# A hybrid recurrent decoder layer on one core: shared buffers, a parameter chain on another engine, and three products or splits moved in the order

## Chip, cores and metric

The kernel runs on one core of a Trainium2 chip. The metric is the device time of one execution in microseconds (us); lower is better. Kernels are compared by the median of several runs.

## The reference, cut to what matters

One layer is computed for 544 tokens of 1024 features in float32: 32 tokens of a sample group (8 sequences of 4) and 512 of a prompt. All the work is on x transposed, features on partitions and tokens along the row.

```python
z = x @ w_in                                   # columns: xa, ya, sb, sc, sh, us, gl
xa_c = conv4(xa);  gx, ga = sigmoid(gates(xa_c))
a = exp(-8 * ga * softplus(-lam)); bx = sqrt(1 - a*a) * gx * xa_c
out_a = (scan(a, bx) * gelu(ya)) @ proj_a      # RG-LRU
out_b = (sb * conv3(sc * sh)) @ proj_b         # short convolution
abar = exp(step * (a_re + i*a_im))             # needs exp, cos, sin of the parameters
y = Re(C @ scan(abar, B @ us)) + d * us        # SSM: 32 groups, 64 complex states each
zc = gelu(y)
out_c = (zc * sigmoid(zc @ glu_w + glu_b)) @ proj_c
m = sum over the branches of sigmoid(gl) * out
x = LN(alpha*x + m @ w_out);  x = LN(alpha*x + relu(x @ up)**2 @ down)
```

## The kernel before

Every float32 product is made of three products of rounded halves: a weight block w is split into wh (a cast on ScalarE, lines 114 and 836) and wl = w - wh (VectorE, lines 115 and 837), the input likewise, and TensorE adds wh.xh, wh.xl and wl.xh (line 146). A tile of z is 128 output features: 48 matmuls over 8 blocks of input features and two halves of the tokens. Weights come by DMA on SyncE's queue into three raw buffers (`rawp`) and, split, into four pairs (`wp`); the split of a block is written two tiles ahead of its product.

Large intermediate tiles come from one pool of 14 equal buffers (`slot`, function `stile`); a new tile waits until the buffer that it is given has been read for the last time. Rows for a single tile (`ttile`) share four buffers and products four PSUM buffers (`big`). The program is written in order for all engines, and a planner then orders each engine's own queue: an instruction that its estimate finds ready may go ahead of an earlier one that is not. On the chip each queue then runs strictly in that order. GpSimd and VectorE operations of all helpers show line 238 (`tt`), 242 and 244 (`ts`).

The first stage computes us, then runs a counter `ti` over the tiles of z: 0 to 7 xa and ya in turn, 8 to 11 sb, 12 to 19 sc and sh in turn; 20 to 27 are the tiles of the merge of branch B (`merge_b`), and 28 on those of branch A (`merge7`, which for most pairs of gate tiles uses seven half-size products instead of eight, `pair7`, with sums of weight blocks on GpSimd and sums of x, `Tt0`). After tile `ti` the side work listed for that number is written (`at`, `run_side`):

- 0: `params_ssm`, the SSM parameters on GpSimd: an exponential of 16 columns, sine and cosine of 128 columns (8 angles), then the small tables A and F; 1: `etable`, which doubles a table E of 128 powers seven times, with factors cn and sn out of the scratch tile scr. 1 to 4: `u_move`, DMAs that bring us_t into the layout U.
- 2 to 9: `a_gate` and `a_rec`, 9 to 12 `a_sqrt` and `a_coef`, 13 `a_scan`, 14 to 17 `a_out`: the RG-LRU.
- for each of eight SSM units u: `ssm_w` and `ssm_o` (weights, GpSimd) ahead, `ssm_a` (transposes) at UA, `ssm_b` at UB = UA + 1 (input product, then scans on VectorE with E, then states HP on GpSimd), `ssm_c` at UC = UA + 2 (output product, reads HP).
- 30 to 33: `z_move`, DMAs that bring the SSM outputs Y into zc.

sb is copied from PSUM into its tile sbt by ScalarE (line 718); the copies must be made before the PSUM buffers can be used again. Before branch A's merge, GpSimd subtracts halves of x in place (`t_sum`, into xq), and four `t_put` calls split the results into the Tt tiles. After it comes the GLU of branch C: zh and zl split zc, two products of glu_w, tanh (th), a product with zt = zh + zl, and a split into ch and cl; then branch C's merge, w_out and the MLP, which the change leaves as they are.

Of the kernel before, what the change touches and what calls it, by code (L numbers as in the profile page):

```python
# [33 lines left out]
RAHEAD = 2  # L34
W2 = 1
AH1 = 4
UA = [13, 15, 17, 19, 21, 22, 24, 25]
UB = [a + 1 for a in UA]
UC = [a + 2 for a in UA]
K4_FIRST = {"a": (3,), "c": ()}  # L40


# [22 lines left out]
def kernel(ctx: ExitStack, tc: tile.TileContext, I, O):  # L65
# [171 lines left out]
    def tt(e, o, a, b, op):  # L237
        e.tensor_tensor(o, a, b, op=op)  # L238
# [75 lines left out]
        ts(V, hb[:, 8:12], C("glb"), 0.5, None, MUL)  # L314
        P["hb"] = hb

    def params_ssm():
        step, dn = P["step"], P["dn"]
        mag = stemp(16)
        va = stemp(16)  # L320
        tt(G, va, step, C("are"), MUL)
        precise_exp(G, mag, va, 16, "e1")
        ang = stemp(128).rearrange("p (f j) -> p f j", f=8)
        tt(G, ang[:, 0], step, C("aim"), MUL)
        for m in range(7):
            ts(G, ang[:, m + 1], ang[:, 0], float(4 << m), None, MUL)
        angf = ang.rearrange("p f j -> p (f j)")
        kk = stemp(128)
        t4 = stemp(128)
        ts(G, kk, angf, 2.0 / math.pi, MAGIC, MUL, ADD)  # L330
        ts(G, kk, kk, MAGIC, None, SUB)
        c1 = float(np.float32(int(math.pi / 2 * 2048) / 2048.0))
        c2_ = math.pi / 2 - c1
        e2 = 2.0 ** (math.floor(math.log2(c2_)) - 11)
        c2v = math.floor(c2_ / e2) * e2
        c3 = c2_ - c2v
        for c in (c1, c2v, c3):
            fma(G, angf, kk, -c, angf, t4)
        r2 = stemp(128)
        snf, cnf = stemp(128), stemp(128)  # L340
        sn, cn = (x.rearrange("p (f j) -> p f j", f=8) for x in (snf, cnf))
        tt(G, r2, angf, angf, MUL)
        f = [1.0 / math.factorial(i) for i in range(13)]
        ts(G, snf, r2, f[9], -f[7], MUL, ADD)
        for c in (f[5], -f[3], 1.0):
            tt(G, snf, snf, r2, MUL)
            ts(G, snf, snf, c, None, ADD)
        tt(G, snf, snf, angf, MUL)
        ts(G, cnf, r2, -f[10], f[8], MUL, ADD)
        for c in (-f[6], f[4], -f[2], 1.0):  # L350
            tt(G, cnf, cnf, r2, MUL)
            ts(G, cnf, cnf, c, None, ADD)
        ts(G, t4, kk, 0.25, MAGIC, MUL, ADD)
        ts(G, t4, t4, MAGIC, None, SUB)
        ta, tb = stemp(128), stemp(128)
        fma(G, kk, t4, -4.0, kk, ta)
        ts(G, ta, kk, 0.0, 2.0, ALU.max, MUL)
        tt(G, t4, ta, kk, SUB)
        ck = stemp(128)
        ts(G, ck, t4, -1.0, 1.0, MUL, ADD)  # L360
        ts(G, t4, t4, -1.0, 2.0, MUL, ADD)
        tt(G, kk, kk, t4, MUL)
        tt(G, ta, snf, kk, MUL)
        tt(G, tb, cnf, kk, MUL)
        tt(G, cnf, cnf, ck, MUL)
        tt(G, cnf, cnf, ta, SUB)
        tt(G, snf, snf, ck, MUL)
        tt(G, snf, snf, tb, ADD)
# [36 lines left out]
        P.update(A_r=A_r, A_i=A_i, F_r=F_r, F_i=F_i, rho=rho, cn=cn, sn=sn)  # L405

    def etable():
        E_r = stile(shape=(128, 16, 128), name="E_r")
# [135 lines left out]

    def z_move(jj):
        if not ZC:
            ZC.append(stile(shape=(128, 4, 4, NCH), name="zc"))
        zc = ZC[0]
        for s in range(4):
            nc.sync.dma_start(out=zc[32 * jj:32 * jj + 32, :, s], in_=YT[0][32 * s:32 * s + 32, jj:16:4])  # L550

# [81 lines left out]
                S.activation(AQ["r"][:, ct], aT[:, ct], AF.Identity, bias=one[:, 0:1], scale=-1.0)  # L633

    def a_sqrt():
        AQ["q"] = stile(name="q")
        S.activation(AQ["q"], aT, AF.Sqrt, scale=-1.0)

    def a_rec(ct):
        r = AQ["r"][:, ct]  # L640
# [1 line left out]
        tt(V, bx[:, ct], bx[:, ct], r, MUL)  # L642

    def a_coef(ct):
        S.activation(aT[:, ct], AQ["r"][:, ct], AF.Identity, bias=one[:, 1:2], scale=2.0)
        tt(V, bx[:, ct], bx[:, ct], AQ["q"][:, ct], MUL)

    def a_scan():
        tm = s1.tile([128, 4, NB], F32, tag="tm", name="tm")
        prev = C("slh").rearrange("p (c b) -> p c b", c=4)  # L650
        for s in range(4):
            tt(V, tm, aT[:, :, s:TS:4], prev, MUL)
            prev = bx[:, :, s:TS:4]
            tt(V, prev, tm, prev, ADD)
        V.tensor_copy(st_lh[:, :, 0:NB], prev)
        for ct in range(4):
            V.tensor_tensor_scan(bx[:, ct, TS:T], aT[:, ct, TS:T], bx[:, ct, TS:T], 0.0, op0=MUL, op1=ADD)
        V.tensor_copy(st_lh[:, :, NB:NB + 1], bx[:, :, T - 1:T])

    def a_out(ct):  # L660
# [8 lines left out]
    def at(i, f, *a):  # L669
        side.setdefault(i, []).append((f, a))  # L670
# [17 lines left out]
    for ct in range(4):  # L688
# [1 line left out]
        at(2 * ct + 3, a_rec, ct)  # L690
        at(9 + ct, a_coef, ct)
        at(14 + ct, a_out, ct)
    at(0, params_ssm)
    at(1, etable)
    side[9].insert(0, (a_sqrt, ()))
    at(13, a_scan)
    at(UB[7], ssm_state)
# [13 lines left out]
        run_side(ti)  # L711
        ti += 1

    sbt = stile(name="sbt")
    for ct in range(4):
        ps = big()
        z_tile(outs_flat(ps))
# [68 lines left out]
        d, e, f = (x[:, :, n] for x, n in (d, e, f))  # L786
        tt(G, d, e, f, SUB)

    def t_puts():
        a, b = xq  # L790
        return [t_put(x[:, :, n]) for x, n in ((a, N1), (b, N2), (a, N2), (b, N1))]

    def t_make(x):
        sr = srp.tile([128, 2, 4, H2], F32, tag="sr", name="sr")
# [78 lines left out]
    def pair7(X, Tt):  # L873
# [14 lines left out]
        prod(P2, Wa, 512, [x[:, :, N1] for x in X[1]])  # L888
        done(Wa)
        tt(V, t[0][:, N1], P2, p1, ADD)  # L890
        Ws = take()
        P6 = mk()
        prod(P6, Ws, 512, Tx(1))
# [47 lines left out]
    def merge7(kh, kl, k4f, pl, out=None):  # L941
# [11 lines left out]
        for q in range(4):  # L953
            if q in k4f:
                ps = prj()
                t = pair7(X0, Tt0)
            elif q in pl:
                ps, t, g = [], [ttile(T, "t") for _ in range(2)], []
                for e in range(2):
                    g.append(big())  # L960
                    W = take()
                    for k in range(KT):
                        sl = slice(k * 128, k * 128 + 128)
                        mm3(outs_flat(g[e]), k == 0, k == KT - 1, W[0][:, sl], W[1][:, sl], *X(k))
                    done(W)
                    S.copy(two(t[e]), flat(g[e]))
                ps = prj()
            else:
                t = pair7(X0, Tt0)
                ps = prj()  # L970
# [51 lines left out]
    wq["cap"] = 4 + W2  # L1022
    for i in range(4):
        t_sum(i)
    Tt0 = t_puts()
    xq.clear()
    merge7(AQ["ah"], AQ["al"], K4_FIRST["a"], (0,))
    for i in sorted(side):
        run_side(i)

    zf = ZC[0].rearrange("p c s n -> p c (s n)")
    zh, zl = stile(F32R, name="zh"), stile(F32R, name="zl")
    for ct in range(4):
        S.copy(zh[:, ct], zf[:, ct])
        tt(V, zl[:, ct], zf[:, ct], zh[:, ct].bitcast(F32), SUB)
    ch, cl = stile(F32R, name="ch"), stile(F32R, name="cl")
    W = None
    for ct in range(4):
        if ct % 2 == 0:
            W = take()  # L1040
        zt = ttile(T, "zt")
        tt(G, zt, zh[:, ct].bitcast(F32), zl[:, ct].bitcast(F32), ADD)
        ps = big()
        k4(outs_flat(ps), W, ct % 2, zh, zl)
        if ct % 2:
            done(W)
        th = ttile(T, "th")
        S.activation(two(th), flat(ps), AF.Tanh, bias=P["hb"][:, 8 + ct:9 + ct], scale=0.5)
        V.scalar_tensor_tensor(th, th, 1.0, zt, op0=ADD, op1=MUL)
        tv = th.rearrange("p (s n) -> p n s", s=4)  # L1050
        cv, dv = (t[:, ct].rearrange("p (n s) -> p n s", s=4) for t in (ch, cl))
        S.mul(cv, tv, 0.5)
        V.scalar_tensor_tensor(dv, tv, 0.5, cv.bitcast(F32), op0=MUL, op1=SUB)
# [420 lines left out]
```

## Time and profile before

| | us |
|---|---|
| median of 3 runs (lowest, highest) | 903.12 (902.12, 907.25) |
| the profiled execution | 903.31 |
| its span, first to last instruction | 901.5 |
| TensorE busy | 842.1 |
| VectorE busy | 592.0 |
| ScalarE busy | 374.7 |
| GpSimd busy | 365.9 |

PE is TensorE, PEld its weight loads, DVE VectorE, ACT ScalarE, POOL GpSimd, SP SyncE. Times in rows are us from the start of the span; an idle time in square brackets stands ahead of the instruction, with what ended it. A group of rows with one line can be that of a helper, so the names of the tiles tell the place.

### The profile page before, as it was taken

To read this page: it belongs to the slowest core of one execution; us is meant where nothing else is said; L and a number is where in the kernel's file an instruction comes from. 1 tells how busy PE (TensorE), PEld (TensorE's weight loads), DVE (VectorE), ACT (ScalarE), POOL (GpSimd) and SP (SyncE) were. 2 spreads that over 40 slices of the span, in tenths; PEclk is the share of its full clock that TensorE was granted. 3 is DMA by queue.
4 is the path that set the end of the run, shared out by engine and by line. 5 is a ranking of instruction groups with operands and counts; after the bars stand their busy time and mean duration, and the time that the engine had idled before them with its cause. 6 is when DMAs were issued, how large, how long until landed. Compare 5 with 4: busy or idle time off the path is not lost.

```text
span 901.5 us, 16029 instructions
## 1 busy us (share of the span) xinstructions
PE 842.1 (93%) x6516; PEld 832.1 (92%) x6516; DVE 592.0 (66%) x888; ACT 374.7 (42%) x616; POOL 365.9 (41%) x442
## 2 busy tenths in 40 slices
PE   7999339899999989979999999999999999999996
PEld 7999339889999989979999899999999999999996
DVE  6767129868465456678866789766665656655657
ACT  4445034432433244354534777444444444444410
POOL 2599971776663744563300311222222222222122
PEclk9999759999999999999999999999999999999999
DMA  8441103212222434312375354323232323233302
GB/s 300 147 120 53 47 1 104 73 54 76 83 72 71 158 85 129 95 53 95 100 251 164 117 187 141 114 94 98 90 99 86 103 87 102 81 107 114 121 1 100
DMA packets 31593, 93.99 MB, mean 104 GB/s; under 512 B 3424, under 2 KB 9952, under 8 KB 31136
## 3 DMA queue, kind: packets, MB, share of 16 engines
q1 hardware_dynamic: 31232, 91.92, 32.2%
q8 instruction: 51, 0.84, 0.4%
q0 software_dynamic: 288, 1.05, 0.3%
q14 instruction: 22, 0.18, 0.1%
HBM read 88.24 MB, written 2.49 MB: 101 GB/s over the span
## 4 chain that ended last, share of the span: by engine, by line
PE 67%; POOL 14%; DVE 10%; issue 3%; ACT 3%; DMA 2%; SPq 0%; DVEq 0%; ACTq 0%; POOLq 0%
PE big L146 40%; PE big L871 21%; POOL scr L238 3%; DVE wl L115 2%; POOL Et L238 2%; POOL sr L238 2%; POOL scr L242 1%; DMA raw<-in_w_dram 1%; PE big L1301 1%; PE big L1142 1%; POOL xq L238 1%; POOL HP L238 1%; ACT wh L114 1%; POOL scr L244 1%; DMA xraw<-in_xT_dram 1%
## 5 line engine op out<-in xcount | busy, mean ns | idle before, releaser
L238 POOL TENSOR_TENSOR sr<-raw 128x512 f32<-128x512 f32 x38 | 62.9, 1675 | 243.4 <-DMA raw<-in_w_dram 217.3
L146 PE MATMUL big<-xh,wh 128*128 128x272 f32 (+2 forms) x544 | 116.5, 296 | 33.3 <-ACT sbt L718 28.7
L115 DVE TENSOR_TENSOR wl<-raw,wh 128x1024 fp32r<-128x1024 f32 x70 | 89.8, 1287 | 48.6 <-ACT wh L114 48.5
L871 PE MATMUL big<-Tt,wh 128*128 128x272 f32 x608 | 116.7, 289 | 3.6 <-DVE uu L238 1.8
L146 PEld LDWEIGHTS big<-xh,wh 128*128 128x128 f32 x544 | 86.7, 192 | 33.8 <-ACT sbt L718 28.9
L114 ACT CAST wh<-raw 128x1024 fp32r<-128x1024 f32 x70 | 73.0, 1048 | 106.0 <-PE big L146 81.4
L146 PE MATMUL big<-xh,wl 128*128 128x272 f32 (+2 forms) x544 | 113.8, 291 | 1.4 <-DVE wl L837 1.4
L146 PE MATMUL big<-xl,wh 128*128 128x272 f32 (+2 forms) x544 | 114.2, 292 | 0.0
L837 DVE TENSOR_TENSOR wl<-raw,wh 128x1024 fp32r<-128x1024 f32 (+1 forms) x73 | 93.0, 1274 | 18.0 <-ACT wh L836 17.1
L836 ACT CAST wh<-raw 128x1024 fp32r<-128x1024 f32 (+1 forms) x73 | 68.4, 937 | 84.0 <-PE big L146 40.5
L871 PEld LDWEIGHTS big<-Tt,wh 128*128 128x128 f32 x608 | 95.6, 188 | 4.2 <-DVE uu L238 2.0
L146 PE MATMUL big<-fh,wh 128*128 128x272 f32 (+2 forms) x448 | 98.2, 289 | 1.0 <-ACT rl L1195 1.0
L146 PE MATMUL big<-fh,wl 128*128 128x272 f32 (+2 forms) x448 | 97.9, 288 | 0.0
L146 PE MATMUL big<-fl,wh 128*128 128x272 f32 (+2 forms) x448 | 97.7, 288 | 0.0
L871 PE MATMUL big<-Tt,wl 128*128 128x272 f32 x304 | 88.2, 290 | 0.0
L146 PEld LDWEIGHTS big<-xh,wl 128*128 128x128 f32 x544 | 86.0, 192 | 1.6 <-DVE wl L837 1.6
L146 PEld LDWEIGHTS big<-xl,wh 128*128 128x128 f32 x544 | 86.5, 192 | 0.1
L837 DVE TENSOR_TENSOR wl<-sr,wh 128x1024 fp32r<-128x1024 f32 x38 | 48.2, 1270 | 45.7 <-ACT wh L836 45.7
L836 ACT CAST wh<-sr 128x1024 fp32r<-128x1024 f32 x38 | 39.6, 1044 | 82.2 <-POOL sr L238 70.6
L146 PEld LDWEIGHTS big<-fh,wh 128*128 128x128 f32 x448 | 72.3, 188 | 1.2 <-ACT rl L1195 1.2
L146 PEld LDWEIGHTS big<-fl,wh 128*128 128x128 f32 x448 | 72.4, 188 | 0.0
L146 PEld LDWEIGHTS big<-fh,wl 128*128 128x128 f32 x448 | 72.0, 189 | 0.0
(292 smaller groups left out, 2089.7 us busy)
## 6 DMA issues: line engine op xcount, KB each, us to landing
raw<-in_w_dram SPq DMA_DIRECT2D x147, 512.0 KB, 3.6
xq<-in_xT_dram SPq DMA_DIRECT2D x2, 1088.0 KB, 6.7
xraw<-in_xT_dram SPq DMA_DIRECT2D x3, 544.0 KB, 7.7
raw<-in_w_dram SPq DMA_DIRECT2D x3, 384.0 KB, 6.8
x<-in_xT_dram SPq DMA_DIRECT2D x2, 576.0 KB, 5.6
U<-us_t SPq DMA_DIRECT2D x16, 68.0 KB, 2.9
zc<-Y SPq DMA_DIRECT2D x16, 68.0 KB, 3.6
bc<-in_bc_dram SPq DMA_DIRECT2D x8, 128.0 KB, 2.8
```

The lines of the kernel that those rows point to most:

```text
L114: S.copy(h, r)
L115: V.tensor_tensor(l, r, h.bitcast(F32), op=SUB)
L146: PE.matmul(out, w, x[:, a:b], start=first and oi == 0, stop=last and oi == 2)
L238: e.tensor_tensor(o, a, b, op=op)
L242: e.tensor_scalar(o, a, s0, None, op0=op0)
L244: e.tensor_scalar(o, a, s0, s1_, op0=op0, op1=op1)
L836: S.copy(h[:, 0:n], src)
L837: V.tensor_tensor(l[:, 0:n], src, h[:, 0:n].bitcast(F32), op=SUB)
L871: PE.matmul(out, w[:, sl], y[:, k], start=k == 0 and oi == 0, stop=k == 3 and oi == 2)
L1142: PE.matmul(out, x, w[:, sl], start=first and kk == 0 and oi == 0, stop=kk == K - 1 and oi == 2)
L1301: PE.matmul(out[:, 256 * e:256 * e + 256], x, w[:, sl], start=False, stop=e == 1 and k == 3 and oi == 2)
```

## The change

1. sbt no longer takes a buffer of its own, but the one of us_t. `a_sqrt` writes its root over aT, and `a_coef` writes 2r - 1 over r; q is gone, and `a_scan` reads r.
2. The exponential, sine and cosine (`params_trig`) are computed by VectorE. The small tables (`params_af`) stay on GpSimd, and `etable` stands ahead of them at 0.
3. Units start one tile earlier for most u, and for the first four the output product is at UA + 3.
4. The four `t_put` are written after the projection's product in the first step of branch A's merge (`t_next`).
5. In the GLU, the product reads zc itself, each tile's split into ch and cl is written behind the next tile's product (`c_split`, through `pend`; the last one within the first `pair7` of branch C's merge), and cl takes zc's buffer.

```diff
-UA = [13, 15, 17, 19, 21, 22, 24, 25]
+UA = [12, 14, 16, 18, 20, 22, 23, 25]
 UB = [a + 1 for a in UA]
-UC = [a + 2 for a in UA]
+UC = [a + (2 if a > 18 else 3) for a in UA]
...
-    def params_ssm():
-        step, dn = P["step"], P["dn"]
+    def params_trig():
+        step = P["step"]
...
-        tt(G, va, step, C("are"), MUL)
-        precise_exp(G, mag, va, 16, "e1")
+        tt(V, va, step, C("are"), MUL)
+        precise_exp(V, mag, va, 16, "e1")
...
-        for c in (c1, c2v, c3):
-            fma(G, angf, kk, -c, angf, t4)
+        for c in (c1, c2v, c3):
+            fma(V, angf, kk, -c, angf, t4)
...
+        P.update(mag=mag, cn=cn, sn=sn)
+
+    def params_af():
+        mag, dn, cn, sn = (P[n] for n in ("mag", "dn", "cn", "sn"))
...
     def z_move(jj):
         if not ZC:
-            ZC.append(stile(shape=(128, 4, 4, NCH), name="zc"))
-        zc = ZC[0]
+            ZC.append(stile(F32R, shape=(128, 4, 4, NCH), name="zc"))
+        zc = ZC[0].bitcast(F32)
...
     def a_sqrt():
-        AQ["q"] = stile(name="q")
-        S.activation(AQ["q"], aT, AF.Sqrt, scale=-1.0)
+        S.activation(aT, aT, AF.Sqrt, scale=-1.0)
...
-        S.activation(aT[:, ct], AQ["r"][:, ct], AF.Identity, bias=one[:, 1:2], scale=2.0)
-        tt(V, bx[:, ct], bx[:, ct], AQ["q"][:, ct], MUL)
+        r = AQ["r"][:, ct]
+        S.activation(r, r, AF.Identity, bias=one[:, 1:2], scale=2.0)
+        tt(V, bx[:, ct], bx[:, ct], aT[:, ct], MUL)
...
-    at(0, params_ssm)
-    at(1, etable)
+    at(0, params_trig)
+    at(0, etable)
+    at(0, params_af)
...
-    sbt = stile(name="sbt")
+    sbt = us_t.rearrange("p c s n -> p c (s n)")
...
+    def t_next():
         a, b = xq
-        return [t_put(x[:, :, n]) for x, n in ((a, N1), (b, N2), (a, N2), (b, N1))]
+        x, n = ((a, N1), (b, N2), (a, N2), (b, N1))[len(Tt0)]
+        Tt0.append(t_put(x[:, :, n]))
+        if len(Tt0) == 4:
+            xq.clear()
...
         tt(V, t[0][:, N1], P2, p1, ADD)
+        while pend:
+            pend.pop()()
...
                 ps = prj()
+                while len(Tt0) < 4:
+                    t_next()
...
-    Tt0 = t_puts()
-    xq.clear()
+    Tt0 = []
...
-    ch, cl = stile(F32R, name="ch"), stile(F32R, name="cl")
+    ch, cl = stile(F32R, name="ch"), ZC[0].rearrange("p c s n -> p c (s n)")
+
+    def c_split(ct, th):
+        tv = th.rearrange("p (s n) -> p n s", s=4)
+        cv, dv = (t[:, ct].rearrange("p (n s) -> p n s", s=4) for t in (ch, cl))
+        S.mul(cv, tv, 0.5)
+        V.scalar_tensor_tensor(dv, tv, 0.5, cv.bitcast(F32), op0=MUL, op1=SUB)
+
...
-        zt = ttile(T, "zt")
-        tt(G, zt, zh[:, ct].bitcast(F32), zl[:, ct].bitcast(F32), ADD)
...
-        V.scalar_tensor_tensor(th, th, 1.0, zt, op0=ADD, op1=MUL)
-        tv = th.rearrange("p (s n) -> p n s", s=4)
...
+        V.scalar_tensor_tensor(th, th, 1.0, zf[:, ct], op0=ADD, op1=MUL)
+        while pend:
+            pend.pop()()
+        pend.append(lambda ct=ct, th=th: c_split(ct, th))
```

## Rows read from the trace of the kernel before

**Rows 1.** Page, part 1: busy us (share of the span) xinstructions of TensorE and its loads.
```profile
PE 842.1 (93%) x6516; PEld 832.1 (92%) x6516; DVE 592.0 (66%) x888; ACT 374.7 (42%) x616; POOL 365.9 (41%) x442
```

**Rows 2.** Waits of TensorE, whole span: engine, line, for whom; us in total, times, longest.
```profile
PE big L146 <- ACT sbt L718: 28.7, 1, 28.7
...
PE big L538 <- POOL HP L238: 3.6, 3, 2.0
PE big L146 <- DVE rl L238: 2.7, 1, 2.7
PE big L539 <- POOL HP L238: 2.7, 3, 1.2
PE big L871 <- ACT t L966: 2.2, 2, 1.8
PE big L871 <- DVE uu L238: 1.8, 1, 1.8
PE big L871 <- ACT th L1048: 1.8, 1, 1.8
PE big L871 <- DVE rl L238: 1.4, 1, 1.4
PE big L146 <- DVE wl L837: 1.4, 1, 1.4
```

**Rows 3.** ScalarE in order of time around 126 us: start, us, operation, [idle before, releaser].
```profile
126.72 0.61 ACT L718 COPY sbt<-big 128x544 f32<-128x544 f32 x1 [35.05 <-POOL Et L238]
```

**Rows 4.** GpSimd in order of time, 30 to 130 us: four points of its chain.
```profile
30.36 0.40 POOL L238 TENSOR_TENSOR scr<-scr,cp 128x16 f32<-128x16 f32 x2 [7.95 <-DVE scr L238]
...
68.19 0.67 POOL L238 TENSOR_TENSOR A_i<-scr 128x16 f32<-128x16 f32 x1
...
97.20 0.13 POOL L411 MEMSET E_r<- 128x16 f32 x1
...
126.77 2.36 POOL L238 TENSOR_TENSOR E_i<-Et 128x1024 f32<-128x1024 f32 x1
```

**Rows 5.** Four stretches: us, then busy us (instructions) of PE, PEld, DVE, ACT, POOL; clock, DMA.
```profile
86.50:98.70 12.20, 12.18 (x91) 11.65 (x89) 5.99 (x4) 1.15 (x2) 11.26 (x22) 1.00 0.27 86
98.70:127.40 28.70, 0.01 (x1) 0.01 (x1) 0.00 (x0) 0.68 (x2) 26.79 (x37) 0.55 0.00 0
127.40:153.80 26.40, 26.40 (x193) 26.40 (x194) 24.31 (x34) 17.32 (x25) 1.73 (x1) 0.90 0.16 47
153.80:173.20 19.40, 16.12 (x130) 15.72 (x129) 18.11 (x31) 8.52 (x21) 13.66 (x15) 1.00 0.37 116
```

**Rows 6.** Chain of waits in order of time: start, us, engine, line, instructions.
```profile
127.39 26.57 PE big L146 x192
...
211.55 9.11 PE big L146 x72
```

**Rows 7.** SyncE's queue in order of time: its last DMAs from us_t.
```profile
48.31 3.31 SPq L583 DMA_DIRECT2D U<-us_t  x4
```

**Rows 8.** VectorE by shape, 20 to 200 us: operation xcount | busy, mean ns.
```profile
L238 DVE TENSOR_TENSOR scr<-scr 128x20 f32<-128x20 f32 x8 | 1.4, 179 | 0.2
L238 DVE TENSOR_TENSOR xx<-X,E_r 128x512 f32<-128x512 f32 x2 | 1.4, 692 | 0.1
```

**Rows 9.** GpSimd by shape, 28 to 130 us, columns as in rows 8.
```profile
L238 POOL TENSOR_TENSOR scr<-scr 128x128 f32<-128x128 f32 x21 | 11.5, 558 | 0.3
...
L238 POOL TENSOR_TENSOR wt<-wt,sp 128x256 f32<-128x256 f32 x2 | 3.3, 1652 | 0.2
...
L238 POOL TENSOR_TENSOR wt<-F_r,bc 128x256 f32<-128x256 f32 x2 | 1.2, 618 | 0.0
...
L238 POOL TENSOR_TENSOR Et<-E_r,scr 128x128 f32<-128x128 f32 x2 | 0.8, 406 | 0.2
```

**Rows 10.** ScalarE in order of time around 317 us, columns as in rows 3.
```profile
317.17 2.11 ACT L778 CAST Tt<-xq 128x1088 fp32r<-128x1088 f32 x2 [6.40 <-POOL xq L238]
```

**Rows 11.** VectorE in order of time around 398 us.
```profile
398.50 1.80 DVE L1049 SCALAR_TENSOR_TENSOR th<-th,zt 128x544 f32<-128x544 f32 x1
```

More of the change, by code (lines that the diff above doesn't have):

```diff
@@ L315, in params @@
         P["hb"] = hb
-    def params_ssm():
-        step, dn = P["step"], P["dn"]
+    def params_trig():
+        step = P["step"]
         mag = stemp(16)
         va = stemp(16)
-        tt(G, va, step, C("are"), MUL)
-        precise_exp(G, mag, va, 16, "e1")
+        tt(V, va, step, C("are"), MUL)
+        precise_exp(V, mag, va, 16, "e1")
         ang = stemp(128).rearrange("p (f j) -> p f j", f=8)
-        tt(G, ang[:, 0], step, C("aim"), MUL)
+        tt(V, ang[:, 0], step, C("aim"), MUL)
         for m in range(7):
-            ts(G, ang[:, m + 1], ang[:, 0], float(4 << m), None, MUL)
+            ts(V, ang[:, m + 1], ang[:, 0], float(4 << m), None, MUL)
         angf = ang.rearrange("p f j -> p (f j)")
@@ L329, in params_ssm @@
         t4 = stemp(128)
-        ts(G, kk, angf, 2.0 / math.pi, MAGIC, MUL, ADD)
-        ts(G, kk, kk, MAGIC, None, SUB)
+        ts(V, kk, angf, 2.0 / math.pi, MAGIC, MUL, ADD)
+        ts(V, kk, kk, MAGIC, None, SUB)
         c1 = float(np.float32(int(math.pi / 2 * 2048) / 2048.0))
@@ L341, in params_ssm @@
         sn, cn = (x.rearrange("p (f j) -> p f j", f=8) for x in (snf, cnf))
-        tt(G, r2, angf, angf, MUL)
+        tt(V, r2, angf, angf, MUL)
         f = [1.0 / math.factorial(i) for i in range(13)]
-        ts(G, snf, r2, f[9], -f[7], MUL, ADD)
+        ts(V, snf, r2, f[9], -f[7], MUL, ADD)
         for c in (f[5], -f[3], 1.0):
[L346 to L349, printed above, removed]
+            tt(V, snf, snf, r2, MUL)
+            ts(V, snf, snf, c, None, ADD)
+        tt(V, snf, snf, angf, MUL)
+        ts(V, cnf, r2, -f[10], f[8], MUL, ADD)
         for c in (-f[6], f[4], -f[2], 1.0):
[L351 to L354, printed above, removed]
+            tt(V, cnf, cnf, r2, MUL)
+            ts(V, cnf, cnf, c, None, ADD)
+        ts(V, t4, kk, 0.25, MAGIC, MUL, ADD)
+        ts(V, t4, t4, MAGIC, None, SUB)
         ta, tb = stemp(128), stemp(128)
-        fma(G, kk, t4, -4.0, kk, ta)
-        ts(G, ta, kk, 0.0, 2.0, ALU.max, MUL)
-        tt(G, t4, ta, kk, SUB)
+        fma(V, kk, t4, -4.0, kk, ta)
+        ts(V, ta, kk, 0.0, 2.0, ALU.max, MUL)
+        tt(V, t4, ta, kk, SUB)
         ck = stemp(128)
[L360 to L368, printed above, removed]
+        ts(V, ck, t4, -1.0, 1.0, MUL, ADD)
+        ts(V, t4, t4, -1.0, 2.0, MUL, ADD)
+        tt(V, kk, kk, t4, MUL)
+        tt(V, ta, snf, kk, MUL)
+        tt(V, tb, cnf, kk, MUL)
+        tt(V, cnf, cnf, ck, MUL)
+        tt(V, cnf, cnf, ta, SUB)
+        tt(V, snf, snf, ck, MUL)
+        tt(V, snf, snf, tb, ADD)
+        P.update(mag=mag, cn=cn, sn=sn)
+    def params_af():
+        mag, dn, cn, sn = (P[n] for n in ("mag", "dn", "cn", "sn"))
         A_r = const.tile([128, 16, 4], F32, name="A_r")
@@ L404, in params_ssm @@
             cmul(F_r[:, :, s], F_i[:, :, s], F_r[:, :, 3], F_i[:, :, 3], A_r[:, :, 2 - s], A_i[:, :, 2 - s])
-        P.update(A_r=A_r, A_i=A_i, F_r=F_r, F_i=F_i, rho=rho, cn=cn, sn=sn)
+        P.update(A_r=A_r, A_i=A_i, F_r=F_r, F_i=F_i, rho=rho)
     def etable():
@@ L644, in a_coef @@
     def a_coef(ct):
-        S.activation(aT[:, ct], AQ["r"][:, ct], AF.Identity, bias=one[:, 1:2], scale=2.0)
-        tt(V, bx[:, ct], bx[:, ct], AQ["q"][:, ct], MUL)
+        r = AQ["r"][:, ct]
+        S.activation(r, r, AF.Identity, bias=one[:, 1:2], scale=2.0)
+        tt(V, bx[:, ct], bx[:, ct], aT[:, ct], MUL)
     def a_scan():
+        a_ = AQ.pop("r")
         tm = s1.tile([128, 4, NB], F32, tag="tm", name="tm")
@@ L651, in a_scan @@
         for s in range(4):
-            tt(V, tm, aT[:, :, s:TS:4], prev, MUL)
+            tt(V, tm, a_[:, :, s:TS:4], prev, MUL)
             prev = bx[:, :, s:TS:4]
@@ L656, in a_scan @@
         for ct in range(4):
-            V.tensor_tensor_scan(bx[:, ct, TS:T], aT[:, ct, TS:T], bx[:, ct, TS:T], 0.0, op0=MUL, op1=ADD)
+            V.tensor_tensor_scan(bx[:, ct, TS:T], a_[:, ct, TS:T], bx[:, ct, TS:T], 0.0, op0=MUL, op1=ADD)
         V.tensor_copy(st_lh[:, :, NB:NB + 1], bx[:, :, T - 1:T])
@@ L787, in t_sum @@
         tt(G, d, e, f, SUB)
-    def t_puts():
+    def t_next():
         a, b = xq
-        return [t_put(x[:, :, n]) for x, n in ((a, N1), (b, N2), (a, N2), (b, N1))]
+        x, n = ((a, N1), (b, N2), (a, N2), (b, N1))[len(Tt0)]
+        Tt0.append(t_put(x[:, :, n]))
+        if len(Tt0) == 4:
+            xq.clear()
     def t_make(x):
@@ L1029 @@
         run_side(i)
-    zf = ZC[0].rearrange("p c s n -> p c (s n)")
+    zf = ZC[0].bitcast(F32).rearrange("p c s n -> p c (s n)")
     zh, zl = stile(F32R, name="zh"), stile(F32R, name="zl")
@@ L1048 @@
         S.activation(two(th), flat(ps), AF.Tanh, bias=P["hb"][:, 8 + ct:9 + ct], scale=0.5)
-        V.scalar_tensor_tensor(th, th, 1.0, zt, op0=ADD, op1=MUL)
-        tv = th.rearrange("p (s n) -> p n s", s=4)
-        cv, dv = (t[:, ct].rearrange("p (n s) -> p n s", s=4) for t in (ch, cl))
-        S.mul(cv, tv, 0.5)
-        V.scalar_tensor_tensor(dv, tv, 0.5, cv.bitcast(F32), op0=MUL, op1=SUB)
+        V.scalar_tensor_tensor(th, th, 1.0, zf[:, ct], op0=ADD, op1=MUL)
+        while pend:
+            pend.pop()()
+        pend.append(lambda ct=ct, th=th: c_split(ct, th))
     mh, ml = ([stile(F32R, name=n) for _ in range(2)] for n in ("mh", "ml"))
```

## The prediction

> **What bounds the kernel now.** I read the page first: TensorE is busy for 842.1 of 901.5 us [rows 1]. No other engine is near that, and none of the edits takes a product away, so what the change can give is bounded by TensorE's idle time, 59 us. Next I asked for TensorE's waits over the whole span [rows 2]. One wait is half of the idle time: 28.7 us, once, for ScalarE's copy into sbt (line 718). Six short ones, 3.6 + 2.7 = 6.3 us, are for HP, the SSM states that the output product reads. Four (1.4, 2.2 in two and 2.7, together 6.3) lie around the start of the second projection (lines 837, 966 and the first rl), and three more (1.8, 1.4, 1.8, together 5.0: th, the second rl, uu) around the GLU. These four groups are what the diff touches.
>
> For the long wait I read who stands behind it. ScalarE's copy starts at 126.72 and had waited 35.05 us for an Et operation of GpSimd [rows 3]; the table is built in place with factors out of scr, so the buffer that sbt was given was still being read. GpSimd's own order [rows 4] says why so late: the parameter chain starts at 30.36, the trigonometry is over when A_i is formed at 68.19, the small tables and the first unit's weights last to 97.20, and the doubling table E from there to 126.77 + 2.36 = 129.13. So the kernel's first 130 us have a serial GpSimd chain in them, and TensorE hits it at 98.7.
>
> The stretches [rows 5] show what the wait did to the others: in 98.7 to 127.4 VectorE did nothing (0.00) and TensorE's granted clock was 0.55, near its lower level of 1.2 GHz; in the 26.4 us after it VectorE was busy for 24.31, catching up. TensorE started slowly as well. In the chain of waits the 192 matmuls after the wait took 26.57 us, while 72 such matmuls at the full clock take 9.11 [rows 6]; 192 would take 24.3, so the slow start cost 2.3.
>
> **The change part by part.**
>
> *sbt in the buffer of us, sqrt and 2r - 1 in place.* sbt then needs no new buffer. The last reader of us_t is the group of DMAs into U that ends its issue at 48.31 + 3.31 = 51.6 [rows 7], some 40 us before sbt is written, so the copy waits for TensorE's product alone. The wait of 28.7 goes, and the slow start of 2.3 with it: 31.0. The two in-place edits have the same operations with the same sizes; each only ties ScalarE's 2r - 1 to VectorE's product with r, hidden behind four tiles of products. Cost: nothing, and if that cover is gone, what the next point but one prices.
>
> *Trigonometry on VectorE.* It takes 37.8 us on GpSimd (30.36 to 68.19 [rows 4]). Counted in the diff it is 31 operations of 16 columns and 41 of 128. No row has such an operation of 128 columns on VectorE; the nearest are 20 columns at 179 ns and 512 at 692 [rows 8], so 128 columns lie between 179 and 692, and on the line between them at 292 ns. Sum: 31 x 0.179 + 41 x 0.292 = 17.5; with all at 0.179 it is 12.9. VectorE also has weight splits and the first convolution in that time, so I take 20 for the stretch (my choice; 13 to 24). TensorE is fully fed just before the long wait (12.18 of 12.20 us in 86.5 to 98.7 [rows 5]), and by the code weights have four buffers, so they are split up to three tiles ahead: I cost this on VectorE at nothing. The cover is those three tiles (18 us, at 6.1 each [rows 6]); without it the 20 us would stand on TensorE's path less what VectorE idles.
>
> *When the tables are ready.* Trigonometry ends at 30.4 + 20 = 50.4. I keep GpSimd's order of before for the rest: 97.20 - 68.19 = 29.0 for small tables and first weights, to 79.4. Then E. Its 31.9 us of before fell into the stretch in which VectorE was idle [rows 5], and now VectorE will be working. What that costs is seen in one shape at two places [rows 9]: 128 x 128 products took 558 ns beside a busy VectorE and 406 beside an idle one, a factor of 1.37. The bounds are 1 and the worst pair there, 1652 against 618 ns, 2.67. With 1.37 E is done at 79.4 + 43.7 = 123; with 1 at 111; with 2.67 at 165. Who needs it: without the wait TensorE goes on at 98.7, has four tiles (24.3) and a little SSM work, so ssm_b(0) brings E's first reader at about 125. The table comes just in time.
>
> *VectorE in the same stretch.* From 86.5 on it has what it had in 86.5 to 98.7 and in 127.4 to 173.2: 5.99 + 24.31 + 18.11 = 48.4 us of work [rows 5], for which there will be 12.2 + (26.4 - 2.3) + (19.4 - 3.3) = 52.4 us. It fits with 4 us to spare, and GpSimd's table now runs beside the 24.31 that ran alone; slowed by a fifth they are 4.9 more. So a wait of some us is likely here, for weights or for a table, in place of the long one. I take 5 for both points together; bounds 0 and 40 (E at 165 against 125).
>
> How far the two engines share is the open point, and the rows speak for sharing in part: in 153.8 to 173.2 they were busy for 18.11 and 13.66 of 19.4 us [rows 5], more together than one after the other would allow, yet with single operations drawn out to 1652 ns. The Trainium skill has a rule that speaks against this edit (SBUF — State Buffer, Who interferes with whom): GpSimd and VectorE share a port pair under an exclusive lock, and whoever comes second is blocked for the other's whole instruction, also when the VectorE instruction reads two operands from SBUF. By it the table and VectorE's work would add up, which is rival R1; by the factor 1.37 the sum below stands at 866, by adding up at 877.
>
> *SSM output product two tiles behind.* Before, ssm_c(u) is queued one tile (48 matmuls, 6.1 us) after ssm_b(u) and then waits up to 2.0 + 1.2 us for HP. One tile more is longer than that wait, so the 6.3 us go, for the four units that had it; a late table (above) makes HP late too, so I count 5.3. Bounds 0 and 6.3. Later units already have longer steps between and keep their place.
>
> *Sums of x split behind a projection.* Before, ScalarE's Tt casts stand in its queue ahead of the copy that frees the PSUM of the first two tiles (line 966), and two of them waited 6.40 us for GpSimd's subtractions [rows 10]. TensorE's 2.2 us are that wait passed on, and part of the 1.4 may be. Behind the projection in the program the casts come later, but the order on ScalarE is made by a planner that fills free time, and it may put them where they were. The same casts free the buffer that zc needs, and zc's DMAs stand in SyncE's queue ahead of weight loads: the 2.7 could grow. I take 2.5 of 6.3; bounds -3 and 6.3.
>
> *GLU.* zt's four GpSimd sums go, th of one tile is split behind the next tile, and cl takes zc's buffer. The waits come of VectorE's order in that stretch: th's product at 398.50 took 1.80 us and stood behind a split of the tile before and ahead of the rl that TensorE waited for [rows 11]. With the split behind it, two of the three waits should shrink. I take 3.5 of 5.0; bounds 0 and 5.0.
>
> **The sum.** It is made against the profiled execution, 903.31 us (span 901.5 and 1.8 around it), which is 0.2 above the median of the three runs, 903.12; the difference is below what matters. 903.3 - 31.0 - 5.3 - 2.5 - 3.5 + 5 = 866.0 us. The bounds of single terms reach from 854.7 (all gone, no new wait) to 903.3 - 31.0 + 3 + 40 = 915.
>
> **The rivals.**
>
> *R1: table and VectorE add up.* As a mechanism of this kernel: every GpSimd operation of E waits for the VectorE operation before it, and the reverse, so that E ends at 79.4 + 31.9 + 24.3 = 135.6, some 11 us after its first reader's 125, and VectorE is as late with the splits behind it. New waits 11 to 20 in place of 5: 872 to 881, say 877. For it: operations at 1652 ns [rows 9]. Against it: 18.11 and 13.66 in one stretch of 19.4, and TensorE's slack of four PSUM buffers. This is what the lock of the Trainium skill's page (SBUF — State Buffer) would make of the change.
>
> *R2: GpSimd builds E before the small tables*, since the diff puts it first. Then the E table is done at 50.4 + 43.7 = 94 and the first unit's weights wt at 94 + 29 = 123, while TensorE wants them after three tiles, at 117. That is 6 us, and the next units' weights queue behind: new waits 10 to 25, 871 to 886. For it: the program's order. Against it: before, too, the E table stood ahead of the first unit's weights in the program, and GpSimd ran it last [rows 4].
>
> *R3: the long wait goes and the smaller edits give nothing.* HP, x and GLU at zero: 903.3 - 31.0 + 5 = 877. For it: no row shows the planner's new order.
>
> *R4: everything fits.* No new wait, and all four groups gone: 903.3 - 31.0 - 6.3 - 6.3 - 5.0 = 854.7. Against it: VectorE has 4 us to spare.
>
> *R5: the change does not do what it says.* The buffer that sbt had is given to a later tile, bh, whose cast ScalarE queues as well; if it comes ahead of the work that TensorE needs, ScalarE stands before the same table. But bh follows the first short convolution, after 125; it would have to wait 30 us there. Time 903, within 0.5%.
>
> *R6: slower.* E is slowed so far beside a busy VectorE that TensorE waits longer than the 42 us gained: E must end after 125 + 42 = 167, that is 87.6 us for work of 31.9, a factor of 2.75. The worst pair is at 2.67 [rows 9], for two instructions only. With a whole table beyond 2.75 the time is over 903, say 910.
>
> **How the numbers follow.** Main case (new waits 0 to 10, at least half of the small terms: 857 to 872) 0.58; R1 0.13; R2 0.09; R3 0.08; R4 0.05; R5 0.03; R6 0.04. The predicted time is the main case's, 866. Left out of the range are R5 and R6 (0.07), what of R1 and R2 lies above 884 (0.06) and half of R4 (0.03): 854 to 884. A difference under 0.5% (4.5 us) is about what a measurement of this kernel cannot tell from none. Faster 0.93, same 0.03, slower 0.04.
>
> **What would show it.** In the profile after: TensorE's table of waits without sbt; GpSimd's trigonometry gone from 30 to 68 and its E table ending near 120; 72 small VectorE operations between 30 and 54; no HP wait on lines like 538; the clock at 1.00 in the slices at 100 to 130; VectorE nearly full from 90 to 175. The prediction is wrong if TensorE waits over 10 us in 86 to 180 (then R1 or R2, told apart by whether the E table or wt is last on GpSimd), if a new wait for weights appears in the first 100 us (then VectorE's cover was not three tiles), or if the waits around the second projection grow (then the sums of x came too late).

## The result, and the profile after

The changed kernel takes 872.48 us (median of 4 runs, 870.16 to 874.27) against 903.08 for the kernel before in the same call: a ratio of 0.9657, 95% interval 0.9619 to 0.9695. The prediction was 866.0 us in a range of 854 to 884. A second measurement of the same two kernels on another chip gave 871.46 and 0.9631 (0.9602 to 0.9661). The profiled execution took 873.84 us with a span of 871.9, so the span is 29.6 us shorter than before.

The page's first part for the kernel after, columns as in [rows 1]:

```profile
PE 840.8 (96%) x6516; PEld 830.8 (95%) x6516; DVE 609.1 (70%) x960; ACT 373.7 (43%) x616; POOL 336.8 (39%) x366
```

TensorE's busy time is 1.3 us less than before with the same 6516 instructions, and its idle time fell from 59.4 to 31.1 us. VectorE has 72 instructions more, GpSimd 76 fewer. So the gain is idle time of TensorE. The waits of TensorE over the whole span say which, columns as in [rows 2]:

```profile
PE big L146 <- DVE wh L201: 4.6, 1, 4.6
PE big L511 <- ACT W L494: 3.5, 1, 3.5
PE big L146 <- DVE rl L238: 3.0, 1, 3.0
PE big L146 <- DVE wl L846: 2.7, 1, 2.7
PE big L542 <- POOL HP L238: 2.1, 1, 2.1
PE big L880 <- DVE uu L238: 1.8, 1, 1.8
PE big L880 <- DVE rl L238: 1.3, 1, 1.3
PE big L543 <- POOL HP L238: 1.2, 1, 1.2
...
PE big L146 <- DVE bl L238: 1.1, 1, 1.1
PE big L146 <- ACT gy L716: 0.9, 1, 0.9
```

The wait of 28.7 us for sbt is gone. HP is left with one unit's 2.1 + 1.2 us, and three waits are new: W 3.5, bl 1.1, gy 0.9. (The first row is the start of the kernel and was there before.)

GpSimd in order of time shows when the tables were ready; compare [rows 4]:

```profile
46.21 1.35 POOL L238 TENSOR_TENSOR Et<-E_i,scr 128x16 f32<-128x16 f32 x1 [8.94 <-DVE scr L238]
...
96.75 2.87 POOL L238 TENSOR_TENSOR E_i<-Et 128x1024 f32<-128x1024 f32 x1
...
102.87 0.23 POOL L238 TENSOR_TENSOR F_i<-scr 128x16 f32<-128x16 f32 x1
...
105.84 0.74 POOL L238 TENSOR_TENSOR wt<-wt,sp 128x256 f32<-128x256 f32 x1
```

VectorE released GpSimd at 46.2. From there the E table and the small tables were worked off mixed with each other: E was done at 99.6 (before: 129.1), the last reader of scr at 103.1, the first unit's weights at 106.6. Three stretches of 50 us, columns as in [rows 5]:

```profile
0.00:50.00 50.00, 45.40 (x341) 45.18 (x342) 38.05 (x169) 21.18 (x37) 9.68 (x34) 1.00 0.63 206
50.00:100.00 50.00, 49.06 (x366) 47.41 (x365) 38.68 (x30) 23.69 (x42) 50.00 (x75) 1.00 0.30 84
100.00:150.00 50.00, 43.25 (x331) 42.62 (x330) 45.80 (x64) 24.91 (x53) 32.19 (x40) 0.96 0.24 74
```

GpSimd is full from 50 to 100 and no longer afterwards; VectorE is nearly full from 100 to 150 (45.80), and that is where TensorE idles most (43.25 busy). ScalarE in order of time shows how the one follows from the other:

```profile
117.00 0.65 ACT L669 CAST ah<-gy 128x544 fp32r<-128x544 f32 x1 [6.56 <-DVE gy L238]
122.82 0.65 ACT L669 CAST ah<-gy 128x544 fp32r<-128x544 f32 x1 [5.17 <-DVE gy L238]
...
128.12 0.60 ACT L494 COPY W<-big 128x512 f32<-128x512 f32 x1
```

The casts of ah wait for VectorE's scan and product, and the copy into W, whose product TensorE had ended at 119.2, stands behind them. TensorE's 3.5 us end with it, at 128.77.

### The profile page after: what moved, and what is told of

Same layout as the page of the kernel before. It is cut to its first block, busy times and chain, and to the rows that moved or that the text cites. A ratio compares the mean times of both kernels' runs of the same rounds, so it can differ in the third digit from the quotient of the medians.

```text
span 871.9 us, 16022 instructions
## 1 busy us (share of the span) xinstructions
PE 840.8 (96%) x6516; PEld 830.8 (95%) x6516; DVE 609.1 (70%) x960; ACT 373.7 (43%) x616; POOL 336.8 (39%) x366
## 3 DMA queue, kind: packets, MB, share of 16 engines
q0 software_dynamic: 288, 1.05, 0.3%
## 5 line engine op out<-in xcount | busy, mean ns | idle before, releaser
L846 DVE TENSOR_TENSOR wl<-sr,wh 128x1024 fp32r<-128x1024 f32 x38 | 48.9, 1287 | 45.7 <-ACT wh L845 45.6
```

The source lines that it names most:

```text
L846: V.tensor_tensor(l[:, 0:n], src, h[:, 0:n].bitcast(F32), op=SUB)
```

## The experiments

Every ratio is to the kernel before in runs on the same chip. Eleven variants ran, and the kernel after once more: first single parts, then the question of what removed the long wait.

**Only sbt in the buffer of us.** The kernel before with one line changed.

```diff
-    sbt = stile(name="sbt")
+    sbt = us_t.rearrange("p c s n -> p c (s n)")
```

> The kernel before with one edit: sbt in the buffer of us_t. The trigonometry stays on GpSimd, so the E table cannot end earlier than before (129 us). Theory 1 (the wait was for the buffer and the tables were only just late): the 28.7 us wait and its slow start of 2.3 go, and the first reader of E, which now comes at about 125, waits 4 to 12 us for it: 876 to 885. Rival (the move of the trigonometry was needed: without it TensorE waits for tables or weights as long as it did for sbt): 895 to 903. Second rival (the buffer alone is the whole gain): 870 to 873.

Measured: 901.31 us, ratio 0.9939 (0.9908 to 0.997), as the first rival had it: almost the whole gain is missing. ScalarE in order of time:

```profile
127.76 2.02 ACT L637 ACTIVATE q<-aT 128x2176 f32<-128x2176 f32 x1 [30.80 <-POOL Et L238]
```

sbt no longer waits, but q, the square root's tile, is the next to take a buffer that GpSimd reads for E, and stands 30.8 us in ScalarE's queue instead. My theory that this line alone takes the wait away fell.

**sbt, sqrt and 2r - 1, nothing else.** q no longer exists here; the trigonometry stays on GpSimd in its old place.

```diff
+    sbt = us_t.rearrange("p c s n -> p c (s n)")
...
-        AQ["q"] = stile(name="q")
-        S.activation(AQ["q"], aT, AF.Sqrt, scale=-1.0)
+        S.activation(aT, aT, AF.Sqrt, scale=-1.0)
...
+        S.activation(r, r, AF.Identity, bias=one[:, 1:2], scale=2.0)
```

> The kernel before with the whole buffer edit (sbt in us_t's buffer, sqrt and 2r - 1 in place) and nothing else: the trigonometry stays on GpSimd in its old order. Theory 1: the sbt-only run gained little because the wait for scr's old readers went to the next new tile, q; with q gone too no new tile waits for the E table, the copies of ScalarE run, TensorE passes 98.7 us and the next stop is the E table itself, whose first reader is due at about 125. E was done at 129 beside an idle VectorE; beside a working one, at the factor of 1.1 to 1.2 that its wide operations show after the change, at about 133. So a wait of 4 to 12 us is left of the 31: 878 to 886 us, and the trigonometry's place is worth the rest. Rival: the wait goes on to a third tile in the ring and stays at some 15 to 25 us: 893 to 903 us. Second rival: E is needed later than forecast and everything fits: 870 to 876 us, as in the kernel after.

Measured: 896.73 us, 0.9908 (0.9876 to 0.9941): the first rival. ScalarE and VectorE in order of time, then TensorE's waits:

```profile
135.85 1.74 ACT L665 CAST ah<-gy 128x544 fp32r<-128x544 f32 x3 [30.28 <-POOL Et L238]
```

```profile
110.02 0.71 DVE L238 TENSOR_TENSOR gy<-gy,bx 128x544 f32<-128x544 f32 x1
...
138.28 2.18 DVE L238 TENSOR_TENSOR al<-gy,ah 128x544 fp32r<-128x544 f32 x2 [17.14 <-POOL E_i L238]
```

```profile
PE big L146 <- ACT us_t L719: 15.7, 1, 15.7
```

The wait went on to a third tile, ah, and its partner al has one of the same kind. ScalarE came to ah at 105.6, and ah's first input gy was done at 110.7 (110.02 + 0.71); from then on only the buffer was missing, and the copies that free TensorE's PSUM buffers queue behind ah. So the date that matters here is 110.7, when the next new tile could be written, and the whole buffer edit is worth about 8 us while E ends at 138.

**Only the trigonometry, with E queued first.** The kernel before, with sbt and q in buffers of their own; params_trig is that of the change, on VectorE.

```diff
-    at(0, params_ssm)
-    at(1, etable)
+    at(0, params_trig)
+    at(0, etable)
+    at(0, params_af)
```

> The kernel before with one edit: exponential, sine and cosine on VectorE, small tables and the E table as in the changed kernel; sbt keeps its own buffer. In the changed kernel the last reader of scr is done at about 97 us, and ScalarE comes to sbt's copy at 99. Theory 1 (either edit alone takes the long wait away, since an earlier table also frees the buffer): 872 to 880. Rival (sbt is given another buffer that is freed late, so the wait stays): 895 to 903.

Measured: 880.52 us, 0.9708 (0.9683 to 0.9733), 0.5 us above the range of theory 1, whose mechanism held. ScalarE in order of time, and TensorE's wait:

```profile
100.40 0.61 ACT L723 COPY sbt<-big 128x544 f32<-128x544 f32 x1 [8.37 <-POOL E_i L238]
```

```profile
PE big L146 <- ACT sbt L723: 3.1, 1, 3.1
```

With E done at 100.4, the old buffers cost TensorE 3.1 us in place of 28.7. This part alone gives 26.3 us (906.82 - 880.52), of 34.2 that the next run gave on the same chip. It moves two things, the trigonometry and E's place in the program; with the trigonometry on VectorE no run separates them.

**The other way round: the kernel after with sbt in a buffer of its own.**

```diff
-    sbt = us_t.rearrange("p c s n -> p c (s n)")
+    sbt = stile(name="sbt")
```

> The changed kernel with sbt in a buffer of its own again. Theory 1 (the two edits on the long wait are redundant): the same time within 3 us, 870 to 875. Rival (the buffer is what took the wait away): 885 to 900.

Measured: 872.64 us, 0.9626 (0.9596 to 0.9657), no different from the kernel after, as theory 1 had it. Once E is early, the line that names the change is not needed.

**The kernel after with the trigonometry on GpSimd**, first with E queued first as it is there:

```diff
-        tt(V, va, step, C("are"), MUL)
+        tt(G, va, step, C("are"), MUL)
...
```

> The changed kernel with the trigonometry on GpSimd again, everything else as changed. GpSimd then ends the trigonometry at about 68 us in place of 46, so its tables (99.6) and first unit weights (106.6) come some 22 us later, at 122 and 129, while TensorE wants the weights at 117: theory 1, TensorE waits 8 to 14 us there and VectorE is relieved by 15 us of work, so the wait of 3.5 us for W and part of that for HP go: 874 to 882. Rival (VectorE was the bound in this stretch, and the late tables are hidden): 862 to 869.

Measured: 878.12 us, 0.9693 (0.9665 to 0.9722), in the range of theory 1. TensorE's waits, then ScalarE and VectorE in order of time:

```profile
PE big L488 <- POOL wt L238: 14.0, 2, 12.5
```

```profile
121.31 0.65 ACT L669 CAST ah<-gy 128x544 fp32r<-128x544 f32 x1 [14.88 <-POOL F_r L238]
```

```profile
120.51 0.72 DVE L238 TENSOR_TENSOR gy<-gy,bx 128x544 f32<-128x544 f32 x1
```

Now the first unit's weights come last (at 131.8), and TensorE waits for them. The 14.88 us of ah are not a wait for a buffer in effect: its input gy was done at 121.23, 0.1 us before the buffer was free, and no wait of TensorE comes of it. E ended at 120.05 in this run. Then with the small tables ahead of E, as before:

```diff
-    at(0, etable)
     at(0, params_af)
+    at(1, etable)
```

> The kernel after with the trigonometry on GpSimd and the small tables ahead of the E table, as in the kernel before; with the E table first on GpSimd the run that only moved the trigonometry back waited 14 us for the first unit's weights wt and took 878. Theory 1: GpSimd's chain is then the bound whichever comes first; wt is ready at about 97, E at 132 to 137 against a first reader at about 122 to 125: TensorE waits 7 to 15 us for the table, 874 to 882 us. Rival: VectorE, relieved of the trigonometry, is what set the time, and with the tables in this order the wait is hidden: 868 to 873 us, which would make the move to VectorE worth nothing.

Measured: 887.91 us, 0.9804 (0.9774 to 0.9834), slower than either theory had it. TensorE's waits, and ScalarE in order of time:

```profile
PE big L511 <- ACT W L494: 18.1, 1, 18.1
```

```profile
136.43 1.74 ACT L669 CAST ah<-gy 128x544 fp32r<-128x544 f32 x3 [30.31 <-POOL Et L238]
```

The weights are early, E ends at 138.8, and ah stands 30.3 us for a buffer again (its input was done at 111.3). Step by step, then: E's place ahead of the small tables takes the ratio from 0.9804 to 0.9693, some 10 us, and the trigonometry's place, once E is first, from 878.12 to the 872.64 of the run before on the same chip, some 5.5. Whether the buffer or the whole chain of GpSimd is the limit, the next run was to tell.

**The same with no new tile in the stretch.** ah takes aT's buffer and al that of r; a and r are rounded for it, which changes their last bits.

```diff
-            AQ["ah"], AQ["al"] = stile(F32R, name="ah"), stile(F32R, name="al")
+            AQ["ah"], AQ["al"] = aR, AQ.pop("rr")
```

> The run that had the trigonometry on GpSimd and the small tables first (888 us), with one thing more: ah takes the buffer of aT and al that of r (both then written as rounded values, which changes the last bits of a and r), so that no tile that ScalarE or VectorE writes between 95 and 135 us needs a buffer out of which GpSimd still reads. GpSimd's chain stays as it is, E done at about 138 to 139. Theory 1: what the late table costs is the buffers, not its data. Then ScalarE's cast of ah no longer waits 30 us, the copy into W comes at about 125, TensorE's wait of 18 us for W goes, and the next stop is the table's first reader, VectorE's product xx, which came at 136.3 us in the kernel after: VectorE waits 2 to 4 us for E there, TensorE 0 to 6 for HP: 871 to 878 us. Rival: the data of the table is what is late, and a wait of 10 to 18 us shows up for HP or W in place of it: 880 to 888 us.

Measured: 886.54 us, 0.9808 (0.9787 to 0.9829), the same as with the wait for buffers. TensorE's waits, then GpSimd and VectorE in order of time:

```profile
PE big L488 <- POOL wt L238: 14.9, 2, 13.7
...
PE big L511 <- ACT W L494: 0.8, 1, 0.8
```

```profile
140.50 2.56 POOL L238 TENSOR_TENSOR E_i<-Et 128x1024 f32<-128x1024 f32 x1
143.01 1.68 POOL L238 TENSOR_TENSOR wt<-F_r,bc 128x256 f32<-128x256 f32 x2
```

```profile
140.78 0.68 DVE L238 TENSOR_TENSOR xx<-big,E_r 128x512 f32<-128x512 f32 x1
```

The wait for buffers is gone (W 0.8), as theory 1 said, and the time stays: TensorE now waits 13.7 us for the second unit's weights, which GpSimd makes only after E. E itself was done at 143.1, 4.2 us later than with the wait for buffers, since VectorE now worked beside it. E's own reader, xx, comes at 140.8, 4.5 us later than in the kernel after, behind a full VectorE. The time is the rival's, but the wait is for neither HP nor W; theory 1 was right on the buffers and wrong on what comes next. A serial chain on GpSimd that ends past 140 is met at whichever of its products TensorE needs first.

**The small edits, one undone at a time in the kernel after.** The units' old places, so that ssm_c follows one tile behind:

```diff
-UA = [12, 14, 16, 18, 20, 22, 23, 25]
+UA = [13, 15, 17, 19, 21, 22, 24, 25]
...
+UC = [a + 2 for a in UA]
```

> The changed kernel with the SSM units at their old tiles and the output product one tile behind the input product. Theory 1 (the second tile hides HP, and the earlier start costs a wait for W of 3.5 us while VectorE is full): HP waits return (3 to 6 us in all against 3.3), the wait for W goes: within 2 us of the changed kernel, 870 to 875. Rival (the edit is worth the 6.3 us of HP waits): 876 to 880.

Measured: 879.2 us, 0.9716 (0.9686 to 0.9745), the rival's time; its profiled execution has a span of 874.2. TensorE's waits:

```profile
PE big L542 <- POOL HP L238: 3.6, 3, 2.0
PE big L627 <- ACT tx L629: 3.3, 1, 3.3
...
PE big L543 <- POOL HP L238: 2.7, 3, 1.2
```

HP is back at exactly its 6.3 us, W's wait is gone, and one for tx is there instead. The ratios put the edit at some 5 us (0.9716 against 0.9657, of 905) and the spans at 2.3 (874.2 against 871.9). The next run below, on the same chip and with the kernel after's order of work, took 872.0 to 874.0 us in its five runs, and this one 876.1 to 881.5: the sign is shown, and the size lies between 2 and 6 us. The waits do not say where it comes from: HP's 6.3 are 3.0 more than in the kernel after.

The casts of Tt ahead of the projection, all four at once:

```diff
     Tt0 = []
+    while len(Tt0) < 4:
+        t_next()
```

> The changed kernel with the four splits of the sums of x written ahead of the merge of branch A again. In the traces the waits around the start of that merge were 1.4 + 2.2 + 2.7 us before and 2.7 + 3.0 after. Theory 1 (the edit moved the wait from the copy to the weight split and is worth under 1 us): 871 to 875. Rival (it is worth the 2.2 us of waits for the copy and more): 875 to 878.

Measured: 873.28 us, 0.9653 (0.9625 to 0.9682), as the kernel after. The order of work on TensorE, VectorE and ScalarE is the same in both traces: the planner puts the casts in the same places whichever way the program has them. In these runs the edit does nothing, as theory 1 had it.

The GLU as before:

```diff
-        V.scalar_tensor_tensor(th, th, 1.0, zf[:, ct], op0=ADD, op1=MUL)
-        while pend:
-            pend.pop()()
...
+        V.scalar_tensor_tensor(th, th, 1.0, zt, op0=ADD, op1=MUL)
```

> The changed kernel with the old GLU: sums zt on GpSimd, each tile split at once, cl in its own buffer. The waits there were 1.8 + 1.4 + 1.8 us before and 1.3 + 1.8 after. Theory 1: 1.8 us slower, 873 to 876. Rival (GpSimd's four sums also hold back the weight sums behind them): 877 to 880.

Measured: 875.64 us, 0.9681 (0.9653 to 0.9709), in the range of theory 1. One wait of before is back:

```profile
PE big L880 <- ACT th L1060: 1.8, 1, 1.8
```

The interval overlaps that of the kernel after; the 1.8 us of the trace are what this edit can be said to give.

**A lighter VectorE.** The decay's exponential alone on GpSimd, which idles until 46 us.

```diff
-        tt(V, va, step, C("are"), MUL)
-        precise_exp(V, mag, va, 16, "e1")
+        tt(G, va, step, C("are"), MUL)
+        precise_exp(G, mag, va, 16, "e1")
```

> The kernel after with the decay's exponential alone (21 operations of 16 columns) back on GpSimd, which idles until about 46 us there, and the sines on VectorE as before. Theory 1: VectorE is the bound in 84 to 150 us of the kernel after (45.8 of 50 us busy in 100 to 150) and each us taken from it earlier ends the backlog sooner; the 21 operations are some 2 to 4 us of VectorE's time, so ScalarE's copy into W waits 1 to 3 us less: 869 to 872 us against 872.5 for the kernel after. Rival: VectorE had slack until 84 us, so work taken away at 30 to 36 us moves nothing later: 872 to 874 us, the same waits.

Measured: 870.53 us, 0.9616 (0.9587 to 0.9644). The kernel after, run beside it:

> The kernel after once more, unchanged, on the chip and against the same runs of the kernel before as the three others: 871 to 874 us by both theories.

gave 871.46 us, 0.9631 (0.9602 to 0.9661). TensorE's waits in the run with the exponential on GpSimd:

```profile
PE big L542 <- POOL HP L238: 2.9, 1, 2.9
PE big L627 <- ACT tx L629: 2.6, 1, 2.6
```

The copy into W comes at 126.79, against 128.55 in the run beside it, and W's wait is gone, as forecast; but HP (0.9 + 1.3 in the run beside it) and tx take its place. The wait's going can't be put down to the exponential: the run with the old GLU, whose edit lies far behind, shows the same exchange (tx 3.3, HP 3.0 + 1.2, no W), since a TensorE held up at tx, at about 93 us, comes later to W. The intervals overlap almost wholly: no better version is shown.

## Why the prediction came out as it did

The time lies in the range, 6.5 us above the forecast. But the step that carried most of the sum was wrong, and that its 28.7 us went all the same is luck: another part of the change, to which the sum gave no gain, took them away.

*The long wait.* I wrote that sbt in the buffer of us removes the 28.7 us, and costed the in-place edits at nothing. The 28.7 went, but this was not why: the edit with the line alone gave 5.5 us and the whole buffer edit some 8 to 9, since the wait passed on from sbt to q and from q to ah. What removed it is that E ends at 99.6 instead of 129: with that, the old buffers cost 3.1 us, and the kernel after with sbt in a buffer of its own nothing. My rival R5 had the mechanism of the buffer edit alone (the old buffer handed to a later tile) but named bh and put its date after 125; the tiles were q and ah, and ah could be written from 110.7 (116.9 in the kernel after).

*When the tables are ready.* I kept GpSimd's order of before, with E from 79.4 to 123. With E queued ahead of the small tables and the factors ready on VectorE, the planner mixed the two, and E ran from 46.2 to 99.6. So a late E was not put to the test in the form that I forecast. What an E ending at 123 would have cost is an estimate: in the run with the whole buffer edit ah's buffer was free 2.4 us before E's end (135.8 and 138.25), which makes 120.6, while ah's first input is ready at 116.9 and the second at 122.8 in the kernel after; some 4 us on ScalarE, and little or nothing of it on TensorE. The run whose E ended at 120.05 shows no wait of TensorE for a buffer; the one whose E ended at 138.8 shows 18.1 us. R2 priced E first as a loss, by late weights; but the small tables were made between E's operations, and wt was ready at 106.6, 11 us ahead of TensorE's first use at 117.77. With the trigonometry on GpSimd and E first, R2's late weights did come: 14.0 us.

*The first reader of E* was put at 125. It is VectorE's product xx at 136.33. Nearer dates were those of the buffers and of wt.

*The trigonometry's price* was right. The new operations on VectorE, by shape, 28 to 60 us, columns as in [rows 8]:

```profile
L238 DVE TENSOR_TENSOR scr<-scr 128x128 f32<-128x128 f32 x21 | 5.5, 292 | 0.1
...
L242 DVE TENSOR_SCALAR scr<-scr 128x128 f32<-128x128 f32 x13 | 2.6, 227 | 0.0
```

Interpolation gave 292 ns for 128 columns and the trace shows 292 for products, 227 for operations with constants. The stretch was 15.9 us (30.4 to 46.3) against 20 assumed. TensorE has no wait for it in that time, as costed.

*The table beside a busy VectorE.* Its 42 operations sum to 30.2 us in the kernel before and 37.2 in the kernel after, a factor of 1.23; in the run without new tiles, where VectorE was busy for 44.06 of the 45.7 us, 44.0 or 1.46. The forecast's 1.37 lies between, and R1's late table did not come. My argument against R1, that the two engines were busy for more than one after the other would allow, proves nothing: an instruction that stands for the other engine counts as busy. VectorE, then GpSimd, in order of time in the first run with the trigonometry on GpSimd:

```profile
117.88 2.24 DVE L238 TENSOR_TENSOR tm<-r,bx 128x32 f32<-128x32 f32 x1
```

```profile
117.66 2.39 POOL L238 TENSOR_TENSOR E_i<-Et 128x1024 f32<-128x1024 f32 x1
```

A product of this size, 0.22 us at 117.62, took 2.24 and ended 0.07 us after GpSimd's operation. What does not stand is VectorE's reciprocal: the four on r took 3.55 us each in the kernels before and after alike. The Trainium skill's page (SBUF — State Buffer, Who interferes with whom) states just this of its exclusive lock: a VectorE instruction with two inputs from SBUF contends with a GpSimd instruction that reads SBUF, and one with at most one such input, outside the two-port modes, does not. The rows here agree. So R1 was too strong in letting all of VectorE's work take turns with the table. The bound of 2.67 was no pair either: it set two different operations side by side, and wt<-wt,sp took 0.74 us at 105.84 above, which makes 1652 ns a factor of 2.2.

*The terms of the sum.* Each by the rows of before and after:

| term | forecast | measured | from |
|---|---|---|---|
| wait for sbt | -28.7 | -28.7 | gone |
| slow start | -2.3 | -1.3 | TensorE busy 842.1 to 840.8 |
| HP | -5.3 | -3.0 | 6.3 to 2.1 + 1.2 |
| sums of x | -2.5 | -0.6 | 6.3 to 3.0 + 2.7 |
| GLU | -3.5 | -1.9 | 5.0 to 1.8 + 1.3 |
| new waits | +5 | +5.5 | W 3.5, bl 1.1, gy 0.9 |
| sum | -37.3 | -30.0 | span: -29.6 |

The terms account for the span to 0.4 us. HP was mis-sized by 2.3: the first unit still waits, since its xx and xy come late from a full VectorE. Sums of x was mis-sized by 1.9: I named the doubt that the planner puts the casts where they were, counted 2.5 all the same, and the run with the old order shows that nothing moved. The wait for t is gone in the trace after, but also in that run, and the second profile of the very same kernel has it with 2.5 us and wl with 1.0 in place of 2.7: the waits around this start trade places from execution to execution, and their sum there (rl 2.5, wl 1.0, t 2.5) is 6.0. The clock: TensorE's granted clock is 1.00 in 100 to 128.7 us, up to the end of the wait for W, and 0.90 in 128.7 to 150, so part of the slow start came back behind that wait.

*VectorE in 86 to 150* was forecast to fit with 4 us to spare and some waits, 5 us taken. That it is the bound there is read from the trace (45.80 of 50 busy, and the chain gy, ah, W); that lightening it helps was tried once and not shown. Of the signs that I named, two did not come: E ended at 99.6 and not near 120, and 3.3 us of waits for HP are left.

## What to carry to other kernels

When an engine waits for a buffer, taking that one tile out of the pool moves the wait to the next tile that asks for it: find the late reader and the date at which any tile of the pool could next be written (its engine free, its input there), and bring the reader ahead of that date. For a serial chain on one engine, list all its products with the dates at which each is needed, buffers included, since removing one meeting point shows the next. Before pricing an edit of program order, ask whether the planner will follow it: here one such swap (E before the small tables, with the trigonometry on GpSimd) was worth some 10 us, 878 against 888, and another (the casts of Tt) nothing.

## What the runs showed of the hardware that was not expected

GpSimd's element-wise operations of one shape were drawn out unevenly beside VectorE. GpSimd in order of time in the kernel after:

```profile
73.10 1.05 POOL L238 TENSOR_TENSOR Et<-E_r,scr 128x512 f32<-128x512 f32 x1
...
76.95 2.03 POOL L238 TENSOR_TENSOR Et<-E_r,scr 128x512 f32<-128x512 f32 x1
```

The same operation took 1.05 us and then 2.03. VectorE in the same stretch says what stood beside each:

```profile
73.45 3.55 DVE L644 RECIPROCAL r<-r 128x544 f32<-128x544 f32 x1 [1.29 <-ACT r L637]
76.92 1.16 DVE L115 TENSOR_TENSOR wl<-raw,wh 128x1024 fp32r<-128x1024 f32 x1
```

The first ran beside the reciprocal, which reads one tile, at the 1.05 us that it takes in the kernel before beside an idle VectorE. The second began 0.03 us after VectorE's split, which reads two, and was longer by 0.98, about the rest of the split's 1.16. So in these rows it is what VectorE does beside an operation that sets its price. The sum over the 42 operations of the table was 1.23 times the undisturbed one in the kernel after and 1.46 times at most in the runs above; it is the sum that a forecast can go by, not the worst single row.
